# A hybrid decoder block on one core: MLP row tiles at another address, the start of the input norm in another order

## The chip, the cores and the metric

One Trainium2 chip, one NeuronCore of it. The metric is the device time of one execution in microseconds; of several runs the median is given. Five engines work side by side, each through its own list of instructions in order: TensorE (PE in the profile, PEld its weight loads), VectorE (DVE), ScalarE (ACT), GpSimd (POOL) and SyncE (SP, here only the queue that issues transfers). They wait for one another by semaphores.

## What is computed

One layer on a sequence of 512 rows of width 1024, float32 in and out:

```python
u = rmsnorm(h, norm_mix_pre_w)
proj = u @ w_in                       # q, k, v, z, xbc, dt_raw, gate_logits
att = dilated_window_attention(q, k, v) @ w_att_proj
ssm = mamba2_mixer(z, xbc, dt_raw, ...) @ w_ssm_proj    # a = -exp(a_log), dt from softplus(dt_raw + dt_bias)
g_att, g_ssm = split(sigmoid(gate_logits + b_gate))
h = h + rmsnorm((g_att * att + g_ssm * ssm) @ w_out, norm_mix_post_w)
f = rmsnorm(h, norm_ffn_pre_w)
f = square(relu(f @ w_up)) @ w_down   # 1024 -> 4096 -> 1024
h = h + rmsnorm(f, norm_ffn_post_w)
```

## The kernel before

**Products in three parts.** A float32 operand is split into a high part in a rounded format (names with h: `uh`, `wh_...`) and a remainder in the same format (names with l: `ul`, `wl_...`). ACT makes the high part by a copy, DVE (at places POOL) the remainder by a subtraction. A product is then three products of TensorE: high x high, high x remainder, remainder x high. One operand of each is loaded into the array and held (128 x 128), the other is streamed through (up to 512 columns).

**Weights.** They come in units of 1 MB into `ws` (two buffers) and are split into `wh` and `wl` (two buffers each). The order of the units is one list; a unit is loaded when the one two places ahead has been used.

**The start.** The 512 rows of x are four tiles of 128 rows, i = 0 to 3. For each, `square_u(i)` makes the mean square (ACT squares and sums; for tiles 0 and 1 ACT takes one half of the columns and DVE the other), and POOL raises it to the power -1/2. `norm_u(i)` multiplies on DVE, in two halves, for tiles 1 to 3 also by the norm's weight row (`row0`, which comes by transfer). `transpose_u` turns the eight 128 x 128 blocks on TensorE (`ut`), and `split_u0`/`split_u` cast them into `uh` and `ul`. Beside this run the first products, the attention values: `values(d, i)` multiplies tile i by the 256 columns of weight unit v1 (d = 1), then v0 (d = 0, with 32 columns more for dt), then v2, in eight steps k of three products each, into banks `psv`. The weights of v1 come in four quarters, and `split_v1(k)` splits the quarter for steps k and k + 1. The table `V_STEPS` says behind which step of which values the norm (n), the squares (s), the transposes (t) and others of later tiles are written. TensorE's list, and the instructions wrapped in `pin`, keep the order in which they are written; the rest is ordered by priority, the earlier written first.

Ahead of all this TensorE multiplies a tile of ones by itself `WARM` times into a bank `warm` that nobody reads. Each such product of 128 x 128 in full float32 is two pieces in the profile.

The small rows `dt_bias` and `a_log` come by transfer into `rows`; ACT takes the exponential of the second (L452). It isn't pinned.

**Middle.** Attention over 12 heads with the other input projections between (psq, psk, psga, psgs, psz), then the state-space mixer by eight groups (psx, psbc, pssp and small products), then the output projection (pso, psp).

**The MLP.** `fh` and `fl` hold the normed rows, transposed, for the up projection (psu, psuX and others). Its result stays in `hidden`, 32 tiles k of 128 features by 512 rows. For the down projection (psd) `hsplit(k)` splits one such tile into `hh` and `hl`; these rows are the operand held in the array, four slices of 128 rows each, and the weights `wh_dn` and `wl_dn` are streamed, 512 columns at a time, into eight banks (four row tiles by two halves). That makes 32 x 4 x 2 x 3 = 768 products. The last weight unit is split into tiles of its own, `wh_l` and `wl_l`. The tiles of k = 0 (`hs0`) lie in the pool `resid`, the others in the pools `hsplit` and `down`.

**Where the tiles lie.** Pools on one side are stacked: `resid` (residual rows, statistics, two or three scratch tiles), on it `fpool` (`fh`, `fl`), and once `fpool` is closed, in its place `down` (with `wh_l`, `wl_l`, `rowe`, the output tiles) and `hsplit`. `fpool` begins with an unused tile `fgap` of 104 floats, 416 bytes. With it `fh` and `fl` begin 480 bytes past a multiple of 512, as do `uh`, `ul`, the weight tiles `wh` and `wl`, and both operands of the output projection. `hh`, `hl`, `wh_l` and `wl_l` begin 64 bytes past one.

Of the kernel before, what the change touches and what calls it, by code (L numbers as in the profile page):

```python
# [11 lines left out]
F32 = mybir.dt.float32  # L12
F32R = mybir.dt.float32r
AF = mybir.ActivationFunctionType
# [4 lines left out]
P = 128  # L19
# [30 lines left out]
V_STEPS = {(1, 0, 2): (("s", 2),), (1, 0, 5): (("t", 1),), (1, 0, 6): (("n", 2),), (1, 1, 1): (("s", 3),),  # L50
           (1, 1, 3): (("t", 2),), (1, 1, 5): (("n", 3),), (1, 2, 3): (("t", 3), ("w", 0)), (1, 2, 7): (("p", 0),)}

WARM = 13
ATT_UNITS = ("q0", "k0", "ga0", "q1", "k1", "ga1", "q2", "k2", "ga2", "ga3", "gs0", "z0")


# [26 lines left out]
def hybrid_block(ctx: ExitStack, tc: tile.TileContext, a: dict):  # L83
    nc = tc.nc
    act, dve, pool, pe, sp = nc.scalar, nc.vector, nc.gpsimd, nc.tensor, nc.sync
# [75 lines left out]
    def v3(t, k):  # L161
        return t.rearrange("p (k n) -> p k n", k=k)
# [53 lines left out]
    ones = const.tile([P, P], F32, name="ones")  # L216
# [5 lines left out]
    def pin(ins):  # L222
        return tc.keep_in_program_order(ins)

    def mm(*args, **kw):
        tc.keep_in_program_order(pe.matmul(*args, **kw))  # L226
# [7 lines left out]
    def three(ps, wh, wl, uh, ul, start, stop, w_moving=False):  # L234
        if w_moving:
            mm(ps, uh, wh, start=start, stop=False)
            mm(ps, uh, wl, start=False, stop=False)
            mm(ps, ul, wh, start=False, stop=stop)
        else:
            mm(ps, wh, uh, start=start, stop=False)  # L240
            mm(ps, wh, ul, start=False, stop=False)
            mm(ps, wl, uh, start=False, stop=stop)
# [11 lines left out]
    def gbank(name):  # L254
        return psg.tile([P, T], F32, name=name, tag="g")
# [21 lines left out]
    with tc.tile_pool(name="start", bufs=1, reuse_waits="tile") as st:  # L277
# [8 lines left out]
        rows = st.tile([P, 2, SH], F32, name="rows")  # L286
# [28 lines left out]
        def square_u(i):  # L315
            un = uns[i] = st.tile([P, D], F32, name=f"un{i}", tag="un", bufs=2)
            if i < 2:
                pin(act.activation(un[:, :T], xt[:, i, :T], AF.Square, scale=RD, accum_out=sq0[:, i, 0:1]))
                pin(dve.tensor_scalar(sq0[:, i, 1:2], sq0[:, i, 0:1], EPS, None, ALU.add))
                pin(dve.tensor_tensor_reduce(un[:, T:], xt[:, i, T:], xt[:, i, T:], 1.0 / D, sq0[:, i, 1:2], ALU.mult,  # L320
                                             ALU.add, rs[:, i : i + 1]))
            else:
                pin(act.activation(un, xt[:, i, :], AF.Square, scale=RD, accum_out=ssq[:, i : i + 1]))
                pin(dve.tensor_scalar(rs[:, i : i + 1], ssq[:, i : i + 1], EPS, None, ALU.add))
            pin(pool.tensor_tensor(rs[:, i : i + 1], rs[:, i : i + 1], mhalf, op=ALU.pow))
# [10 lines left out]
        def transpose_u(i, b, banks=1):  # L336
            pt = [abank(f"ut{i}_{b}{n}") for n in range(banks)]
            for j in range(4):
                k = 4 * b + j
                tr(pt[j % banks][:, j * P : (j + 1) * P], uns[i][:, k * P : (k + 1) * P])  # L340
            pts[i, b] = pt[0]
            for j in range(4):
                pts[4 * b + j] = pt[j % banks][:, j * P : (j + 1) * P]

        def split_u0(k):
            hi = uh[:, k, 0:P]
            pin(act.activation(hi, pts[k], AF.Copy, scale=ncol[:, k : k + 1]))
            pin(dve.scalar_tensor_tensor(ul[:, k, 0:P], pts[k], ncol[:, k : k + 1], hi.bitcast(F32), op0=ALU.mult,
                                         op1=ALU.subtract))

        def split_u(i, b):
            p3 = pts.pop((i, b)).rearrange("p (k t) -> p k t", k=4)
            hi = uh[:, 4 * b : 4 * b + 4, i * P : (i + 1) * P]
            pin(act.activation(hi, p3, AF.Copy))
            pin(dve.tensor_tensor(ul[:, 4 * b : 4 * b + 4, i * P : (i + 1) * P], p3, hi.bitcast(F32), op=ALU.subtract))

        def split_v1(k, eng=dve):
            ks = slice(k * UC, (k + 2) * UC)
            pin(act.activation(wh1[:, ks], ws1[:, ks], AF.Copy))
            pin(eng.tensor_tensor(wl1[:, ks], ws1[:, ks], wh1[:, ks].bitcast(F32), op=ALU.subtract))  # L360

        def split_v0(k, eng=dve):
            ks = slice(k, k + 4)
            pin(act.activation(wh0[:, ks, :], ws0[:, ks, :], AF.Copy))
            pin(eng.tensor_tensor(wl0[:, ks, :], ws0[:, ks, :], wh0[:, ks, :].bitcast(F32), op=ALU.subtract))

        warm = gbank("warm")
        for _ in range(WARM):
            mm(warm[:, 0:P], ones, ones, start=True, stop=True)
        square_u(0)  # L370
        norm_u(0)
        transpose_u(0, 0, 2)
# [1 line left out]
        split_v1(0)  # L374
        split_u0(0)
        split_u0(1)
        square_u(1)
        split_v1(2)
        split_u0(2)
        split_u0(3)  # L380
        split_v1(4, pool)
        split_u0(4)
        split_u0(5)
        norm_u(1, (0,))
# [15 lines left out]
        def values(d, i):  # L400
            isl = slice(i * P, (i + 1) * P)
            n = VW if d == 0 else UC
            hi, lo = (wh0, wl0) if d == 0 else wv[d]
            ps = gbank(f"psv{d}_{i}")
            for k in range(KD):
                three(ps[:, :n], hi[:, k, :], lo[:, k, :], uh[:, k, isl], ul[:, k, isl],
                      k == 0, k == KD - 1, w_moving=True)
                yield
            act.activation(vtok[:, i, d * UC : (d + 1) * UC], ps[:, :UC], AF.Copy)
            if d == 0:  # L410
                dve.tensor_tensor(raw[:, i, :], ps[:, UC:VW], rows[:, 0, :], op=ALU.add)

        wv = {1: (v3(wh1, KD), v3(wl1, KD))}
        for d, i in V_ORDER:
            for k, _ in enumerate(values(d, i)):
                for step, n in V_STEPS.get((d, i, k), ()):
                    if step == "t":
                        transpose_u(n, 0)
                        transpose_u(n, 1)
                        split_u(n, 0)  # L420
                        split_u(n, 1)
                    elif step == "w":
                        split_v0(0)
                        split_v0(4, pool)
                    elif step == "p":
                        prep(0, 0)
                        wv[2] = [v3(t, KD) for t in take("v2")]
                    else:
                        (square_u if step == "s" else norm_u)(n)
# [19 lines left out]
        dve.tensor_scalar(t[0], t[0], 0.0, None, ALU.max)  # L449
        dve.scalar_tensor_tensor(dtp, t[3], 2.0, t[0], op0=ALU.mult, op1=ALU.add)  # L450

        act.activation(rows[:, 1, :], rows[:, 1, :], AF.Exp)  # L452
        for c in range(NT):
            dve.scalar_tensor_tensor(t[1][:, :, c, :], dtp[:, :, c, :], -1.0,
                                     rows[:, 1, :].rearrange("p (g h) -> p g h", g=GROUPS),
# [165 lines left out]
    for key in ATT_UNITS:  # L621
        n, j = key[:-1], int(key[-1])
# [303 lines left out]
    rp = ctx.enter_context(tc.tile_pool(name="resid", bufs=1, reuse_waits="tile"))  # L926
# [5 lines left out]
    rowf = ow.tile([P, D], F32, name="rowf", tag="rowf")  # L932
    sp.dma_start(rowf, a["norm_ffn_pre_w"].broadcast_to([P, D]))
    sm = rp.tile([P, 6, NT], F32, name="sm")

    fctx = ExitStack()
    fp = fctx.enter_context(tc.tile_pool(name="fpool", bufs=1, reuse_waits="tile"))
    fp.tile([P, 104], F32, name="fgap")
    fh = fp.tile([P, KD, T], F32R, name="fh")
    fl = fp.tile([P, KD, T], F32R, name="fl")  # L940

# [414 lines left out]
```

## Time and profile before

| | |
|---|---|
| median of 3 runs | 1108.18 us (1108.18 to 1108.34) |
| the profiled execution's own time | 1107.94 us |
| its span, first to last instruction | 1106.2 us |
| TensorE busy | 1092.2 us, 99% |
| VectorE, ScalarE, GpSimd busy | 726.7, 534.2, 63.8 us |
| mean granted TensorE clock | 0.998 |
| the down product's 768 products, first to last | 920 to 1099.5 us of the span |

A row of the chain of work reads: start, length, engine, tile, line, and how many instructions it holds; a row of groups: line, engine, operation, output<-inputs, shapes, count, then busy time and mean duration in ns, then the idle time of the engine ahead of them. The inputs' names stand in no particular order. A row of the timeline has start and length in us, and in brackets how long the engine was idle before it and what ended that. A row of windows has the stretch, its length, then for each engine (PE, PEld, DVE, ACT, POOL) its busy time and count, then the granted clock, the share of the transfer engines and GB/s. Products overlap, so the duration of one (near 390 ns) is longer than the step to the next (near 230 ns).

### The profile page before, as it was taken

The page shows a single profiled execution, that of the slowest core. Times are in us where ns is not written, and L with a number is a line of the kernel's source. Part 1 is how long each engine was busy: PE and PEld are TensorE (multiplying, and loading weights), DVE is VectorE, ACT ScalarE, POOL GpSimd, SP SyncE. Part 2 cuts the span into 40 slices and gives each one's busy share as a digit, 9 for nine tenths or more (in the row PEclk, how much of TensorE's full clock was granted, in tenths as well). Part 3 has the DMA queues.
Part 4 walks back from the last instruction along what each step waited for, and adds up shares of the span by engine and source line. Part 5 has one row for each costly group of instructions (what it writes and reads, how often), then busy time and mean ns, then how long its engine had stood idle before and what let it go on. Part 6 is the DMA issues. An engine that isn't in the chain of part 4 may idle for free.

```text
span 1106.2 us, 14632 instructions
## 1 busy us (share of the span) xinstructions
PE 1092.2 (99%) x5923; PEld 923.3 (83%) x5923; DVE 726.7 (66%) x1080; ACT 534.2 (48%) x943; POOL 63.8 (6%) x71
## 2 busy tenths in 40 slices
PE   8999999999999999999999999999999999999997
PEld 7988887778878888888888888889899998888886
DVE  5657666446776879696969695868577775332324
ACT  6356656445375654637373723454356764322211
POOL 2203222000000000000000000000000000000000
PEclk9999999999999999999999999999999999999999
DMA  8232222323323232332424223540323333232202
GB/s 276 80 103 81 58 66 67 105 68 104 115 77 115 77 114 77 115 99 93 136 80 127 77 79 112 192 150 2 114 85 107 116 115 133 77 136 93 87 29 76
DMA packets 86756, 110.92 MB, mean 100 GB/s; under 512 B 4240, under 2 KB 74384, under 8 KB 85664
## 3 DMA queue, kind: packets, MB, share of 16 engines
q1 hardware_dynamic: 85216, 101.01, 28.7%
q0 software_dynamic: 1328, 8.98, 2.1%
q8 instruction: 46, 0.75, 0.3%
q14 instruction: 22, 0.18, 0.1%
q10 hardware_dynamic: 144, 0.00, 0.0%
HBM read 107.82 MB, written 2.16 MB: 99 GB/s over the span
## 4 chain that ended last, share of the span: by engine, by line
PE 90%; DVE 4%; ACT 2%; DMA 2%; issue 1%; SPq 1%; POOL 0%; POOLq 0%; DVEq 0%; ACTq 0%
PE psd L226 16%; PE psz L226 8%; PE psx L226 8%; PE pssp L226 7%; PE psbc L226 6%; PE psuX L226 5%; PE psu L226 5%; PE psga L226 4%; PE psgs L226 4%; PE psk L226 3%; PE psq L226 3%; PE psap L226 3%; PE psv L226 3%; PE psuZ L226 3%; PE pq L226 1%; PE pyd L226 1%
## 5 line engine op out<-in xcount | busy, mean ns | idle before, releaser
L226 PE MATMUL psd<-wh_dn,hl 128*128 128x512 f32 x240 | 95.1, 396 | 0.0
L226 PE MATMUL psd<-wl_dn,hh 128*128 128x512 f32 x240 | 95.1, 396 | 0.0
L226 PE MATMUL psd<-wh_dn,hh 128*128 128x512 f32 x240 | 95.1, 396 | 0.0
L98 DVE TENSOR_TENSOR hl<-hidden,hh 128x512 fp32r<-128x512 f32 x32 | 21.9, 692 | 77.8 <-ACT hh L95 77.8
L95 ACT ACTIVATE hh<-hidden 128x512 fp32r<-128x512 f32 x32 | 19.8, 629 | 98.3 <-PE psd L226 98.2
L226 PEld LDWEIGHTS psd<-wh_dn,hl 128*128 128x128 f32 x240 | 45.2, 188 | 11.0
L226 PEld LDWEIGHTS psd<-wh_dn,hh 128*128 128x128 f32 x240 | 45.2, 188 | 10.9
L226 PEld LDWEIGHTS psd<-wl_dn,hh 128*128 128x128 f32 x240 | 45.2, 188 | 10.9
L226 PE MATMUL psbc<-uh,wh_bc 128*128 128x512 f32 x128 | 52.8, 413 | 0.0
L226 PE MATMUL pssp<-yth,wh_sp 128*128 128x512 f32 x128 | 51.4, 401 | 0.0
L226 PE MATMUL psz<-uh,wh_z 128*128 128x512 f32 x128 | 51.1, 399 | 0.0
L226 PE MATMUL psx<-uh,wl_x 128*128 128x512 f32 x128 | 49.9, 390 | 0.7 <-DVE wl_x L98 0.7
L226 PE MATMUL psx<-uh,wh_x 128*128 128x512 f32 x128 | 50.4, 394 | 0.0
L226 PE MATMUL psz<-uh,wl_z 128*128 128x512 f32 x128 | 50.2, 392 | 0.2 <-DVE wl_z L98 0.2
L686 DVE SCALAR_TENSOR_TENSOR ch<-psx,cw,ch 128x511 f32<-128x511 f32 (+2 forms) x48 | 35.9, 747 | 22.0 <-ACT ch L684 21.3
L226 PE MATMUL pssp<-yth,wl_sp 128*128 128x512 f32 x128 | 50.1, 392 | 0.0
L226 PE MATMUL pssp<-ytl,wh_sp 128*128 128x512 f32 x128 | 49.9, 390 | 0.0
L226 PE MATMUL psz<-ul,wh_z 128*128 128x512 f32 x128 | 49.9, 390 | 0.0
L226 PE MATMUL psbc<-uh,wl_bc 128*128 128x512 f32 x128 | 49.9, 390 | 0.0
L226 PE MATMUL psbc<-ul,wh_bc 128*128 128x512 f32 x128 | 49.8, 389 | 0.0
L226 PE MATMUL psx<-ul,wh_x 128*128 128x512 f32 x128 | 49.8, 389 | 0.0
L98 DVE TENSOR_TENSOR wl_dn<-ws_dn,wh_dn 128x2048 fp32r<-128x2048 f32 (+1 forms) x17 | 34.5, 2040 | 14.9 <-ACT wh_dn L95 14.9
(351 smaller groups left out, 3226.3 us busy)
## 6 DMA issues: line engine op xcount, KB each, us to landing
ws_up<-in_w_up_dram SPq DMA_DIRECT2D x16, 1024.0 KB, 5.6
ws_dn<-in_w_down_dram SPq DMA_DIRECT2D x15, 1024.0 KB, 5.0
ws_z<-in_w_in_dram SPq DMA_DIRECT2D x8, 1024.0 KB, 7.1
ws_x<-in_w_in_dram SPq DMA_DIRECT2D x8, 1024.0 KB, 5.3
w<-acs_d POOLq DMA_DIRECT2D x8, 1024.0 KB, 5.0
ws_bc<-in_w_in_dram SPq DMA_DIRECT2D x16, 512.0 KB, 4.8
ws_sp<-in_w_ssm_proj_dram SPq DMA_DIRECT2D x8, 1024.0 KB, 5.0
ws_ga<-in_w_in_dram SPq DMA_DIRECT2D x4, 1024.0 KB, 5.4
```

Of the source, the lines that this page charges most:

```text
L95: ins = act.activation(hi, src, AF.Copy)
L98: ins = (eng or dve).tensor_tensor(lo, src, hi.bitcast(F32), op=ALU.subtract)
L226: tc.keep_in_program_order(pe.matmul(*args, **kw))
L686: dve.scalar_tensor_tensor(h[:, d:], ps[:, : T - d], cw[:, ct, 3 - d : 4 - d], h[:, d:], op0=ALU.mult, op1=ALU.add)
```

## The change

It has four parts. The unused tile of 104 floats moves from `fpool` to `resid`, which lies under it: `fh` and `fl` stay at their addresses, while `hh`, `hl` (those of k = 0 too), `wh_l`, `wl_l`, the output tiles, `rowe` and the scratch tiles of `resid` move up by 416 bytes, from 64 to 480 past a multiple of 512. Constant products stand between the first value products: one more ahead of the start (`WARM`), and by `WARM_AT` 3, 2 and 2 behind steps 1, 3 and 5 of the first tile. In the input norm `square_u(1)` is written behind the casts of steps 2 and 3, and POOL makes the weight remainder of quarter 2 (steps 2, 3) where it made that of quarter 4. The exponential of `a_log` is pinned, which puts it where it is written.

```diff
--- before.py
+++ after.py
@@ -50,7 +50,8 @@
 V_STEPS = {(1, 0, 2): (("s", 2),), (1, 0, 5): (("t", 1),), (1, 0, 6): (("n", 2),), (1, 1, 1): (("s", 3),),
            (1, 1, 3): (("t", 2),), (1, 1, 5): (("n", 3),), (1, 2, 3): (("t", 3), ("w", 0)), (1, 2, 7): (("p", 0),)}
 
-WARM = 13
+WARM = 14
+WARM_AT = {1: 3, 3: 2, 5: 2}
 ATT_UNITS = ("q0", "k0", "ga0", "q1", "k1", "ga1", "q2", "k2", "ga2", "ga3", "gs0", "z0")
 
 
@@ -365,8 +366,12 @@
             pin(eng.tensor_tensor(wl0[:, ks, :], ws0[:, ks, :], wh0[:, ks, :].bitcast(F32), op=ALU.subtract))
 
         warm = gbank("warm")
-        for _ in range(WARM):
-            mm(warm[:, 0:P], ones, ones, start=True, stop=True)
+
+        def warm_up(n):
+            for _ in range(n):
+                mm(warm[:, 0:P], ones, ones, start=True, stop=True)
+
+        warm_up(WARM)
         square_u(0)
         norm_u(0)
         transpose_u(0, 0, 2)
@@ -374,11 +379,11 @@
         split_v1(0)
         split_u0(0)
         split_u0(1)
-        square_u(1)
-        split_v1(2)
+        split_v1(2, pool)
         split_u0(2)
         split_u0(3)
-        split_v1(4, pool)
+        square_u(1)
+        split_v1(4)
         split_u0(4)
         split_u0(5)
         norm_u(1, (0,))
@@ -413,6 +418,8 @@
         wv = {1: (v3(wh1, KD), v3(wl1, KD))}
         for d, i in V_ORDER:
             for k, _ in enumerate(values(d, i)):
+                if (d, i) == (1, 0):
+                    warm_up(WARM_AT.get(k, 0))
                 for step, n in V_STEPS.get((d, i, k), ()):
                     if step == "t":
                         transpose_u(n, 0)
@@ -449,7 +456,7 @@
         dve.tensor_scalar(t[0], t[0], 0.0, None, ALU.max)
         dve.scalar_tensor_tensor(dtp, t[3], 2.0, t[0], op0=ALU.mult, op1=ALU.add)
 
-        act.activation(rows[:, 1, :], rows[:, 1, :], AF.Exp)
+        pin(act.activation(rows[:, 1, :], rows[:, 1, :], AF.Exp))
         for c in range(NT):
             dve.scalar_tensor_tensor(t[1][:, :, c, :], dtp[:, :, c, :], -1.0,
                                      rows[:, 1, :].rearrange("p (g h) -> p g h", g=GROUPS),
@@ -932,10 +939,10 @@
     rowf = ow.tile([P, D], F32, name="rowf", tag="rowf")
     sp.dma_start(rowf, a["norm_ffn_pre_w"].broadcast_to([P, D]))
     sm = rp.tile([P, 6, NT], F32, name="sm")
+    rp.tile([P, 104], F32, name="gap")
 
     fctx = ExitStack()
     fp = fctx.enter_context(tc.tile_pool(name="fpool", bufs=1, reuse_waits="tile"))
-    fp.tile([P, 104], F32, name="fgap")
     fh = fp.tile([P, KD, T], F32R, name="fh")
     fl = fp.tile([P, KD, T], F32R, name="fl")
 
```

TensorE's list in the first values, from the last product of step 0 on; `psv1_0` is the bank of tile 0, `wh_v1`, `wl_v1` the weights, `uh`, `ul` the rows. Before:

```order
L226 MATMUL psv1_0_209<-wh_v1_109,ul_85 128x256 [waits DVE_49]
L226 MATMUL psv1_0_209<-wh_v1_109,uh_84 128x256 [waits Activation_49]
L226 MATMUL psv1_0_209<-wl_v1_110,uh_84 128x256
L226 MATMUL psv1_0_209<-wh_v1_109,ul_85 128x256 [waits DVE_49]
L226 MATMUL psv1_0_209<-wh_v1_109,uh_84 128x256 [waits Activation_49]
L226 MATMUL psv1_0_209<-wl_v1_110,uh_84 128x256 [waits DVE_49]
```

Now:

```order
L227 MATMUL psv1_0_210<-wh_v1_109,ul_85 128x256 [waits DVE_49]
L227 MATMUL psv1_0_210<-wh_v1_109,uh_84 128x256 [waits Activation_49]
L227 MATMUL psv1_0_210<-wl_v1_110,uh_84 128x256
L227 MATMUL psv1_0_210<-wh_v1_109,ul_85 128x256 [waits DVE_49]
L227 MATMUL warm_127<-ones_70 128x128 x3
L227 MATMUL psv1_0_210<-wh_v1_109,uh_84 128x256 [waits Activation_49]
L227 MATMUL psv1_0_210<-wl_v1_110,uh_84 128x256 [waits Pool_49]
```

Behind step 1 stand three constant products, and the product with the remainder of quarter 2 waits for POOL and not for DVE. (Behind steps 3 and 5 stand two each, and the remainder of quarter 4 now comes from DVE.)

ACT's list at the same place (`un1` is the scratch and later the normed tile 1, `sq0` its sum, `ut0_..` the transposed blocks of tile 0). Before:

```order
L347 ACTIVATE uh_84<-ut0_01_149,ncol_99 128x128 [waits PE_49]
L318 ACTIVATE un1_166,sq0_125<-xt_100 128x512 [waits DMAHW5_49]
L359 ACTIVATE wh_v1_109<-ws_v1_108 128x512 [waits DMAHW4_49]
L347 ACTIVATE uh_84<-ut0_00_148,ncol_99 128x128 [waits DVE_49]
L347 ACTIVATE uh_84<-ut0_01_149,ncol_99 128x128 [waits DVE_49]
L359 ACTIVATE wh_v1_109<-ws_v1_108 128x512 [waits DMAHW7_49]
```

Now:

```order
L348 ACTIVATE uh_84<-ut0_01_150,ncol_99 128x128 [waits PE_49]
L360 ACTIVATE wh_v1_109<-ws_v1_108 128x512 [waits DMAHW4_49]
L348 ACTIVATE uh_84<-ut0_00_149,ncol_99 128x128 [waits DVE_49]
L348 ACTIVATE uh_84<-ut0_01_150,ncol_99 128x128 [waits DVE_49]
L319 ACTIVATE un1_173,sq0_125<-xt_100 128x512 [waits DMAHW5_49]
L360 ACTIVATE wh_v1_109<-ws_v1_108 128x512 [waits DMAHW7_49]
```

The square of tile 1 stands behind a weight cast and two row casts. On DVE its sum, the other half's squares and the remainder of a weight quarter likewise follow two row remainders that stood behind them.

POOL's list (`rs` is raised to the power -1/2; `cw`, `cb` are constants of the convolution). Before:

```order
L325 TENSOR_TENSOR rs_126<-rs_126,mhalf_68 128x1 [waits DVE_49,Pool_49]
L325 TENSOR_TENSOR rs_126<-rs_126,mhalf_68 128x1 [waits DVE_49]
L360 TENSOR_TENSOR wl_v1_110<-ws_v1_108,wh_v1_109 128x512 [waits DMAHW7_49,Activation_49]
L325 TENSOR_TENSOR rs_126<-rs_126,mhalf_68 128x1 [waits DVE_49] x2
L431 TENSOR_SCALAR cw_199<-cw_199 128x128 [waits DMAHW4_49]
L431 TENSOR_SCALAR cb_201<-cb_201 128x32 [waits DMAHW5_49]
```

Now:

```order
L326 TENSOR_TENSOR rs_126<-rs_126,mhalf_68 128x1 [waits DVE_49,Pool_49]
L361 TENSOR_TENSOR wl_v1_110<-ws_v1_108,wh_v1_109 128x512 [waits DMAHW4_49,Activation_49]
L326 TENSOR_TENSOR rs_126<-rs_126,mhalf_68 128x1 [waits DVE_49] x3
L438 TENSOR_SCALAR cw_200<-cw_200 128x128 [waits DMAHW4_49]
L438 TENSOR_SCALAR cb_202<-cb_202 128x32 [waits DMAHW5_49]
```

The weight remainder stands ahead of tile 1's power.

ACT's list where the exponential stood (`ut2_..` and `ut3_..` are the transposed tiles 2 and 3, `vtok` the values evacuated from their banks). Before:

```order
L323 ACTIVATE un3_262,ssq_124<-xt_100 128x1024 [waits DMAHW4_49,DVE_49]
L452 ACTIVATE rows_105<-rows_105 128x32 [waits DMAHW0_49]
L354 ACTIVATE uh_84<-ut2_00_272 128x4x128 [waits PE_49]
L354 ACTIVATE uh_84<-ut2_10_277 128x4x128 [waits PE_49]
L409 ACTIVATE vtok_89<-psv1_1_255 128x256 [waits PE_49]
L354 ACTIVATE uh_84<-ut3_00_314 128x4x128 [waits PE_49]
```

Now, there:

```order
L414 ACTIVATE vtok_89<-psv1_0_210 128x256 [waits PE_49]
L324 ACTIVATE un3_270,ssq_124<-xt_100 128x1024 [waits DMAHW4_49,DVE_49]
L355 ACTIVATE uh_84<-ut2_00_280 128x4x128 [waits PE_49]
L355 ACTIVATE uh_84<-ut2_10_285 128x4x128 [waits PE_49]
L414 ACTIVATE vtok_89<-psv1_1_263 128x256 [waits PE_49]
L355 ACTIVATE uh_84<-ut3_00_322 128x4x128 [waits PE_49]
```

and where it now stands, behind the exponential of dt and between evacuations of values:

```order
L414 ACTIVATE vtok_89<-psv0_2_441 128x256 [waits PE_49]
L414 ACTIVATE vtok_89<-psv0_3_468 128x256 [waits PE_49]
L447 ACTIVATE dt1_619<-dt1_619 128x128 [waits DVE_49]
L459 ACTIVATE rows_105<-rows_105 128x32 [waits DMAHW0_49]
L414 ACTIVATE vtok_89<-psv2_0_495 128x256 [waits PE_49]
L414 ACTIVATE vtok_89<-psv2_1_521 128x256 [waits PE_49]
```

Tile 2's casts follow the square of tile 3 directly; the exponential comes seven evacuations later.

## The prediction

> **What bounds the kernel now.** I read the page's share of busy time first, then the chain that ended last, then the groups of matrix products by shape, and last the first 30 us as a timeline, because the change touches only the start and the addresses of the last stage.
>
> ```profile
> span 1106.2 us, 14632 instructions
> PE 1092.2 (99%) x5923; PEld 923.3 (83%) x5923; DVE 726.7 (66%) x1080; ACT 534.2 (48%) x943; POOL 63.8 (6%) x71
> PE 90%; DVE 4%; ACT 2%; DMA 2%; issue 1%; SPq 1%; POOL 0%; POOLq 0%; DVEq 0%; ACTq 0%
> ```
>
> The kernel is a string of products on TensorE; other engines carry a tenth of the chain. So two things can move the time: the step from one product to the next where TensorE is never kept waiting, and the few waits at the start. The chain gives that step directly, since a piece of it is a stretch of products without a gap (start, length, count):
>
> ```profile
> 244.37 10.88 PE psx L226 x48
> 676.60 16.36 PE psgs L226 x72
> 740.37 5.49 PE psp L226 x24
> 920.17 174.16 PE psd L226 x744
> ```
>
> All four are 512 columns wide in the same number type. One step is 226.7 ns in psx, 227.2 in psgs, 228.8 in psp, but 174.16 / 744 = 234.1 ns in psd, the down product of the MLP. The groups by shape (busy, mean ns of one) say the same in another way:
>
> ```profile
> L226 PE MATMUL psd<-wl_dn,hh 128*128 128x512 f32 x240 | 95.1, 396 | 0.0
> L226 PE MATMUL psd<-wh_l,hh 128*128 128x512 f32 x16 | 6.2, 390 | 0.0
> L226 PE MATMUL psd<-wl_l,hh 128*128 128x512 f32 x16 | 6.3, 394 | 0.0
> L226 PE MATMUL pso<-wh_o,mh 128*128 128x512 f32 x32 | 12.4, 389 | 0.0
> L226 PE MATMUL psbc<-uh,wh_bc 128*128 128x512 f32 x128 | 52.8, 413 | 0.0
> ```
>
> The pso products have the psd's form (weights streamed, rows held) and take 389 ns against 396. What differs is the layout: in pso, psx, psgs and psp both operands begin 480 bytes past a multiple of 512. In psd the streamed wh_dn and wl_dn do so too, but the held hh and hl begin at 64. In the last weight pair both wh_l and hh begin at 64, and those rows, in the same stage, lie between (390 and 394). So the trace shows the dear step with unequal residues, cheaper ones with equal residues.
>
> **The layout's price.** The change puts hh, hl, wh_l and wl_l at 480 like the rest; fh and fl stay where they were. No instruction is added. All 768 products of the stage lie on the chain, with no idle time ahead of them (0.0), so what a step saves the end saves. 744 x (234.1 - 227.0) = 5.3 us; the other 24, part of them the cheaper last pair, give some 0.1. Together 5.4 us. I take 227.0, between psx and psgs, since these are stretches without a break. The ends: psp, with transposes just ahead of it, gives 744 x 5.3 = 3.9 us; psx gives 5.6; if equal residues only bring what the wh_l and wl_l rows show (393 on average, 3 under 396), 768 x 3 ns = 2.3 us. A faster stage needs a new pair of weight tiles every 10.9 us (48 products) and not every 11.2; the psd piece runs 174 us with no other engine in it, so loads and casts have room for these 3%.
>
> The Trainium skill (TensorE: Matmul & The Clock Gate, "Step-by-step: what each phase is for") says the opposite of a layout effect: two independent read ports, one for the streamed operand and one for weights, so "Loading the next tile's weights doesn't steal SBUF read bandwidth from the running matmul." By that rule this part brings 0 and the sum keeps only the start, 1106.7; the rows 396 and 389 for one form disagree with it, or at least show something it leaves out.
>
> **The start: clock and norm of tile 1.** Four windows (length, busy time and count by engine, granted clock):
>
> ```profile
> 8.80:12.21 3.41, 1.97 (x12) 1.48 (x12) 3.11 (x9) 2.86 (x9) 2.19 (x2) 1.00 0.98 332
> 12.21:15.63 3.42, 3.00 (x15) 2.60 (x14) 2.61 (x7) 2.03 (x4) 0.55 (x1) 0.50 1.06 379
> 15.63:19.04 3.41, 3.41 (x30) 3.28 (x30) 2.13 (x5) 1.62 (x4) 0.56 (x1) 1.00 0.63 179
> 916.75:920.16 3.41, 2.53 (x21) 2.33 (x20) 3.41 (x7) 1.45 (x3) 0.00 (x0) 1.00 0.20 41
> ```
>
> TensorE was busy 1.97 of 3.41 us, and in the next window its clock is 0.50; after 3.00 it is 1.00 again. A window with 2.53 later in the kernel is followed by no drop. So somewhere between 1.97 and 2.53 busy lies the point at which the clock falls. The rows of that time:
>
> ```profile
> 1.16 5.17 PE L226 MATMUL warm<-ones 128*128 128x128 f32 x26 [1.16 <-POOL ones L217]
> 6.37 1.09 PE L229 MATMUL ut<-ident,un 128*128 128x128 f32 x8
> 7.72 0.63 ACT L318 ACTIVATE un<-xt 128x512 f32<-128x512 f32 x1
> 8.35 0.62 ACT L359 ACTIVATE wh_v<-ws_v 128x512 fp32r<-128x512 f32 x1
> 8.48 0.15 DVE L319 TENSOR_SCALAR sq<-sq 128x1 f32<-128x1 f32 x1 [0.21 <-ACT un L318]
> 9.51 0.94 POOL L325 TENSOR_TENSOR rs<-rs,mhalf 128x1 f32<-128x1 f32 x1 [3.71 <-DVE rs L320]
> 10.41 1.28 POOL L360 TENSOR_TENSOR wl_v<-ws_v,wh_v 128x512 fp32r<-128x512 f32 x1
> 11.37 0.88 DVE L333 SCALAR_TENSOR_TENSOR un<-xt,rs,row 128x512 f32<-128x512 f32 x1 [0.30 <-issue]
> 13.29 0.74 DVE L333 SCALAR_TENSOR_TENSOR un<-xt,rs,row 128x512 f32<-128x512 f32 x1
> 14.08 1.12 PE L229 MATMUL ut<-ident,un 128*128 128x128 f32 x4 [0.42 <-DVE un L333]
> 14.99 0.69 DVE L355 TENSOR_TENSOR ul<-ut,uh 128x512 fp32r<-128x512 f32 x1 [0.33 <-ACT uh L354]
> 15.87 0.69 DVE L355 TENSOR_TENSOR ul<-ut,uh 128x512 fp32r<-128x512 f32 x1 [0.19 <-ACT uh L354]
> 16.47 1.40 DVE L333 SCALAR_TENSOR_TENSOR un<-xt,rs,row 128x512 f32<-128x512 f32 x2
> ```
>
> Step by step. One more constant product ahead: two more pieces, at 5.17 / 26 = 0.2 us each at most; they end about where the transposes start (6.37), so 0 to 0.1. ACT squares tile 1 behind a weight cast and two row casts, about 0.9 later (8.6 for 7.72), so DVE's row of 8.48 comes at 9.34. DVE works from 8.48 to 11.07 on what precedes the first half of tile 1's norm (11.37, after 0.30 idle); two row remainders of 0.26 each now go ahead of it. 9.34 + 2.59 - 0.52 = 11.41, against 11.37: nothing lost, because the 0.30 of idle covers it; were that cover absent, 0.3 would be. POOL makes the weight remainder (1.28) ahead of its power (0.94): it can begin at 8.2, once ACT has cast them, and end at 9.5, before the power's input comes at 10.3 (9.34 + 0.15 + the 0.75 or so of the other half's squares). TensorE gets its third and fifth weight remainders some 0.6 and 0.8 us earlier.
>
> The seven constant products (14 pieces, some 0.11 us each at full clock, 1.6 in all) stand where TensorE waits anyway: 3 while the third weights are made, 2 and 2 before tile 1's norm. They end before the first half arrives at 12.3, cost nothing on the path, and lift 1.97 above 3. So 12.21 to 15.63 runs at full clock. That is worth little: DVE ends tile 1's norm at 14.07 for 14.03, the four transposes then take 0.55 (half of the 1.09 for eight) for 1.12, and the second DVE remainder can start no sooner than 0.60 behind 14.99: 15.59 for 15.87. Norm of tile 2 and what follows come 0.28 earlier.
>
> **The exponential.**
>
> ```profile
> 18.35 0.36 PE L226 MATMUL psv<-wh_v,uh 128*128 128x256 f32 x1
> 19.49 0.23 ACT L452 ACTIVATE rows<-rows 128x32 f32<-128x32 f32 x1 [1.88 <-DMA rows<-in_a_log_dram]
> 19.63 1.07 ACT L354 ACTIVATE uh<-ut 128x512 fp32r<-128x512 f32 x2
> 20.24 1.29 DVE L355 TENSOR_TENSOR ul<-ut,uh 128x512 fp32r<-128x512 f32 x2 [2.30 <-ACT uh L354]
> 20.26 0.39 PE L226 MATMUL psv<-wh_v,uh 128*128 128x256 f32 x1 [0.24 <-ACT uh L354]
> 20.99 0.39 PE L226 MATMUL psv<-wh_v,ul 128*128 128x256 f32 x1 [0.22 <-DVE ul L355]
> 21.45 1.41 DVE L333 SCALAR_TENSOR_TENSOR un<-xt,rs,row 128x512 f32<-128x512 f32 x2
> 22.28 1.35 PE L229 MATMUL ut<-ident,un 128*128 128x128 f32 x8
> 23.38 0.37 PE L226 MATMUL psv<-wh_v,uh 128*128 128x256 f32 x1
> 26.45 2.80 POOL L365 TENSOR_TENSOR wl_v<-ws_v,wh_v 128x1152 fp32r<-128x1152 f32 x1 [3.49 <-ACT wh_v L364]
> 29.52 0.29 PE L226 MATMUL psv<-wl_v,uh 128*128 128x288 f32 x1
> ```
>
> ACT stands 1.88 us for a small transfer, with tile 2's casts queued behind it; DVE waits 2.30 for them, then TensorE for both. Without the exponential there, ACT casts tile 2 from about 18.3. TensorE would be at the next tile at 18.35 + 12 x 0.12 = 19.8 (the window at 15.63 holds 30 products and transposes in 3.41, 0.11 to 0.12 each), not 20.26 (0.4); its product with the remainder follows 0.24 behind and not at 20.99 (0.5); the transposes of tile 3 no longer wait for DVE's norm (22.28 to 23.38 is 1.1, eight take 0.9: 0.2), and 0.1 of uneven steps goes. With the 0.25 from the clock TensorE reaches the product of 23.38 at 21.9: 1.45 us. What is late next: POOL's weight remainder ends at 29.25 and TensorE uses it at 29.52. It moves along, for it hangs on ACT behind tile 3's transposes; if it did not, 1.2 of the 1.45 would be lost there. In its new place the exponential (0.23) stands on ACT ahead of the evacuations of the last four value tiles. With three banks TensorE needs an evacuated bank only two tiles later, some 5 us; that is its cover, and without it the cost would be 0.23. No DMA is moved, and nothing on SP's queue. Ends for the whole start: 0.3 and 1.7.
>
> **Sum.** Profiled execution 1107.94 (1.74 around its span): 1107.94 - 5.4 - 1.45 = 1101.1. The median of the runs, 1108.18, is 0.24 above that execution, so 1101.3.
>
> **The rivals.** *The clock falls one window later.* From 12.21 to 15.63 TensorE would wait from about 12.9 to 14.1 for the norm: 2.2 busy, between 1.97 and 2.53, the gap in which the drop sits. Then 15.63 to 19.04 is at half clock; working the same rows at twice the step, TensorE is about 0.9 late at 18.35, the exponential's gain absorbs most, and 0.3 stays: 1102.5. For it: those 2.2 are nearer to 1.97. Against: 8 transposes and 8 products run in it at full clock, where the earlier window had 12 products. The Trainium skill (the same page, "Part 4: PE-mode transpose") says that transposes do not count as busy in the same way, which would favour this rival; no row here separates them. That page's table for the clock ("What's actually happening") lets the clock drop only after an idle window; by it neither window would have dropped, and the trace's 1.97 busy followed by 0.50 disagrees.
>
> *Equal residues bring only the last pair's rows.* 2.3 instead of 5.4: 1104.4. For it: that pair is the only one in this stage with equal residues. Against: it is mixed with unequal ones.
>
> *The layout does nothing*, and 234.1 has another cause, such as the stage's transfers and casts: only the start remains, 1106.7. Against it: the wh_l rows at 390 in the same stage.
>
> *Equal residues at 480 are themselves dear* (ends slower). The first product of each triple at 480 takes 413 in psbc. If the down stage took that for a third of its products, 256 x 17 ns = 4.4 us more, less 1.45: 1111.1. It decides from 410 ns on. Against it: pso at 389.
>
> **How the numbers follow.** The forecast 0.50, clock one window later 0.25, last pair's rows 0.10, layout nothing 0.12, 480 dear 0.03. A measurement of this kernel tells about 0.2% (2.2 us) from no change: the first three are faster, 0.85; layout nothing is the same, 0.12; slower 0.03. The range goes from 1100.5 (5.6 and 1.7, without the 0.24) to the last pair's 1104.4, which leaves 0.15 out.
>
> **What would show it.** A psd piece of the chain at 227 ns a step and groups at 389 to 390; no half clock in 12.21 to 15.63, nor after; no wait of ACT on the a_log transfer; the first 288-column product at 26.3 for 27.8. A psd step still at 234, or a half clock at 15.63, makes me wrong.

## The result, and the profile after

| | before | after |
|---|---|---|
| median of 6 runs | 1108.09 us (1107.58 to 1108.34) | 1101.12 us (1100.69 to 1101.41, and one run of 1545.77) |
| the profiled execution's own time | 1107.94 us | 1101.41 us |
| its span | 1106.2 us | 1099.6 us |
| TensorE busy | 1092.2 us | 1086.6 us |

After to before is 0.9937, with a 95% interval of 0.9924 to 0.9951: 7 us less. The run of 1545.77 us had a mean clock of 0.654 over its whole length and stands outside that ratio; the median without it is 1100.99.

The head of the page of after:

```profile
span 1099.6 us, 14665 instructions
PE 1086.6 (99%) x5939; PEld 923.9 (84%) x5939; DVE 725.3 (66%) x1080; ACT 534.5 (49%) x943; POOL 63.9 (6%) x71
```

The same four stretches of the chain as in the prediction (start, length, count), now of after:

```profile
243.21 10.88 PE psx L227 x48
675.52 16.36 PE psgs L227 x72
739.44 5.49 PE psp L227 x24
919.22 168.68 PE psd L227 x744
```

Two differences to read. The psd piece takes 168.68 us for 174.16: one step is 168.68 / 744 = 226.7 ns, the step of psx, so the dear step is gone. And psd starts at 919.22 for 920.17: 0.95 came from the start in this execution. 5.48 + 0.95 is nearly all of the span's 6.6; what stands behind the piece, its last 24 products among it, gives most of the rest. psx, psgs and psp keep their lengths to the last digit.

The groups by shape of after (busy, mean ns of one):

```profile
L227 PE MATMUL psd<-wl_dn,hh 128*128 128x512 f32 x240 | 93.4, 389 | 0.0
L227 PE MATMUL psd<-wh_dn,hl 128*128 128x512 f32 x240 | 93.4, 389 | 0.0
L227 PE MATMUL psbc<-uh,wh_bc 128*128 128x512 f32 x128 | 52.9, 413 | 0.0
```

396 became 389, while psbc's 413, which a rival took for the price of the place 480, stands as it stood.

The start. Rows of after's timeline:

```profile
6.80 1.04 PE L230 MATMUL ut<-ident,un 128*128 128x128 f32 x8
8.55 1.28 POOL L361 TENSOR_TENSOR wl_v<-ws_v,wh_v 128x512 fp32r<-128x512 f32 x1 [2.86 <-ACT wh_v L360]
9.63 0.15 DVE L320 TENSOR_SCALAR sq<-sq 128x1 f32<-128x1 f32 x1 [0.26 <-ACT un L319]
11.63 0.75 DVE L334 SCALAR_TENSOR_TENSOR un<-xt,rs,row 128x512 f32<-128x512 f32 x1
13.42 0.74 DVE L334 SCALAR_TENSOR_TENSOR un<-xt,rs,row 128x512 f32<-128x512 f32 x1
17.71 1.26 ACT L355 ACTIVATE uh<-ut 128x512 fp32r<-128x512 f32 x2 [0.67 <-PE ut L230]
21.83 0.36 PE L227 MATMUL psv<-wh_v,uh 128*128 128x256 f32 x1
26.23 0.30 PE L227 MATMUL psv<-wh_v,uh 128*128 128x288 f32 x1
28.27 0.40 PE L227 MATMUL psv<-wl_v,uh 128*128 128x288 f32 x1
```

ACT casts tile 2 at 17.71, released by the transposes and no longer by the a_log transfer (19.63 before). The product of 23.38 stands at 21.83, the first of 288 columns at 26.23 for 27.78: 1.55 earlier. But the first product that needs POOL's remainder of v0, the fifth with a weight remainder, begins at 28.27, 1.25 earlier than the 29.52 of before; it stands 0.43 us behind the product before it, where the step is 0.13, so 0.3 us are lost there. POOL's rows say why:

```profile
23.65 0.54 POOL L438 TENSOR_SCALAR cw<-cw 128x128 f32<-128x128 f32 x1 [5.33 <-DMA cw<-in_conv_w_dram]
24.16 1.20 POOL L438 TENSOR_SCALAR cb<-cb 128x32 f32<-128x32 f32 x1
25.32 0.25 POOL L438 TENSOR_SCALAR bg<-bg 128x16 f32<-128x16 f32 x1
25.54 2.68 POOL L366 TENSOR_TENSOR wl_v<-ws_v,wh_v 128x1152 fp32r<-128x1152 f32 x1
```

ACT had made the input of L366 by 24.87 (2.22 us from 22.65), but POOL's list has three small products on constants ahead of it, and the transfer of cw came at 23.65; before it came at 21.18.

The granted clock, window by window (length, busy time and count of PE, PEld, DVE, ACT, POOL, clock):

```profile
9.66:13.07 3.41, 3.18 (x23) 2.79 (x23) 3.37 (x10) 2.12 (x6) 1.11 (x2) 1.00 1.02 372
13.07:16.48 3.41, 2.32 (x19) 2.12 (x19) 2.71 (x6) 3.02 (x6) 0.55 (x1) 1.00 1.04 333
16.48:19.90 3.42, 3.42 (x30) 3.18 (x29) 2.77 (x6) 1.86 (x5) 0.55 (x1) 1.00 0.61 195
```

No half clock behind the window of 3.18, and none behind the one of 2.32. The windows are not where they were: in before the clock rose first at 5.39 us of the span, here at 6.24.

### The profile page after: what moved, and what is told of

Read it like the earlier page. It is cut to its first block, busy times and chain, and to the rows that moved or that the text cites. A ratio compares the mean times of both kernels' runs of the same rounds, so it can differ in the third digit from the quotient of the medians.

```text
span 1099.6 us, 14665 instructions
## 1 busy us (share of the span) xinstructions
PE 1086.6 (99%) x5939; PEld 923.9 (84%) x5939; DVE 725.3 (66%) x1080; ACT 534.5 (49%) x943; POOL 63.9 (6%) x71
## 4 chain that ended last, share of the span: by engine, by line
PE 89%; DVE 4%; ACT 2%; DMA 1%; issue 1%; POOL 1%; POOLq 0%; DVEq 0%; ACTq 0%
PE psd L227 15%; PE psz L227 8%; PE psx L227 8%; PE pssp L227 8%; PE psbc L227 6%; PE psuX L227 5%; PE psu L227 5%; PE psga L227 4%; PE psgs L227 4%; PE psk L227 3%; PE psq L227 3%; PE psap L227 3%; PE psuZ L227 3%; PE psv L227 2%; PE pq L227 1%; PE pyd L227 1%
```

## The experiments

Two theories were to be told apart first: that the address of the MLP's rows is the cause of the dear step, and that the start had somehow changed the stage; then which part of the start pays, and what about the address counts.

### Each half by itself

**The layout alone**, on the kernel before:

```diff
     sm = rp.tile([P, 6, NT], F32, name="sm")
+    rp.tile([P, 104], F32, name="gap")
...
-    fp.tile([P, 104], F32, name="fgap")
```

> Only the unused tile of 104 floats moves; the start is that of before. If the address is the cause of the dear step: psd piece of the chain 168 to 169 us (226.7 ns a step), psd start unchanged at 920.2, time 1108.1 - 5.5 = 1102.6. If the layout does nothing and the start changed the stage (for instance by the clock's phase): 174 us in the psd piece, 1108.1. If only like residues of the last pair count: 1105.8.

**The start alone**: the changed kernel with these two lines put back.

> All changes at the start, the layout as before. If the two parts are independent: the psd piece stays at 174.2 us (234.1 ns a step), psd starts at 919.0 to 919.3 where it started at 920.17, time 1108.1 - 1.1 = 1107.0. If the start also acts on the stage: psd piece under 173. The wait for the late remainder at 28 us is expected again if it hangs on the instruction order (first wl_v product with 288 columns at 28.3), and gone (27.9) if it came from one late transfer of that execution.

**The exponential alone**, on the kernel before:

```diff
-        act.activation(rows[:, 1, :], rows[:, 1, :], AF.Exp)
+        pin(act.activation(rows[:, 1, :], rows[:, 1, :], AF.Exp))
```

> Before, with the exponential pinned and nothing else. If the exponential carries the start's gain: no wait of ACT on a_log, the first 288-column product at 26.6 for 27.78 and psd start at 919.2 to 919.5, time 1107.2. If most of the gain came from the clock window (half clock from 12.2 to 15.6 before): psd start 920.0, time 1107.9.

The last piece of the chain (start, length, count), with the layout alone:

```profile
920.70 168.68 PE psd L226 x744
```

With the start alone:

```profile
918.79 174.16 PE psd L227 x744
```

And with the exponential alone:

```profile
918.94 174.16 PE psd L226 x744
```

| | median, us | to before (1107.95, 21 runs) | ratio, 95% |
|---|---|---|---|
| layout alone | 1102.54 (5 runs) | -5.41 | 0.9951 [0.9939, 0.9964] |
| start alone | 1106.59 (11 runs) | -1.36 | 0.9987 [0.9978, 0.9996] |
| exponential alone | 1106.70 (11 runs) | -1.25 | 0.9989 [0.998, 0.9998] |

The halves add up, within the noise: 5.41 + 1.36 = 6.77, of the 6.97 measured together. The psd piece is 168.68 with the layout and 174.16 without it, whatever the start. The exponential alone brings 1.25 of the 1.36, and the intervals can't tell these two apart. Both kernels started psd earlier than expected (918.79 for 919.0 to 919.3, 918.94 for 919.2 to 919.5) and ended 0.4 to 0.5 us sooner than expected. The wait of TensorE at 28 us, seen in the changed kernel, is in neither profile. Two more lines, of the timelines, show how the exponential acts. ACT's exponential in the kernel with the layout alone:

```profile
20.02 0.23 ACT L452 ACTIVATE rows<-rows 128x32 f32<-128x32 f32 x1 [2.82 <-DMA rows<-in_a_log_dram]
```

ACT's casts of tile 2 in the kernel with the exponential alone:

```profile
18.11 1.26 ACT L354 ACTIVATE uh<-ut 128x512 fp32r<-128x512 f32 x2 [0.54 <-PE ut L229]
```

The first of these two kernels has the start of before, and ran this time without a half clock in the start. ACT was free earlier, at 17.2 instead of 17.6, and waited 2.82 us instead of 1.88, since the transfer set the time. psd then started even later than in before, 920.70 for 920.17. So full clock ahead of that wait bought nothing in this execution. The runs of before fit it: of the 21, the four with a mean clock of 1.000 took 1107.56 to 1108.48 us, the six with 0.996 or 0.997 took 1107.62 to 1108.76.

### The a_log transfer early

The kernel before, with the transfer on another queue and the exponential pinned at its old place:

```diff
         act.dma_start(ncol, a["norm_mix_pre_c"])
+        act.dma_start(rows[:, 1, :], a["a_log"].broadcast_to([P, SH]))
...
                         (square_u if step == "s" else norm_u)(n)
+                        if (step, n) == ("s", 3):
+                            pin(act.activation(rows[:, 1, :], rows[:, 1, :], AF.Exp))
```

> Before, with a_log loaded at the start on ACT's own queue, behind ncol, and the exponential pinned where it stood, between the square of tile 3 and the casts of tile 2. Nothing else changes. If ACT's wait for that small transfer is the price: exponential at 17.6 without a wait, psd start at 919.1 to 919.4, time as with the pinned exponential plus up to 0.2, 1106.7 to 1107.0. If its place between the casts is the price: 1108.

Measured: 1107.46 us (11 runs), ratio 0.9996 [0.9987, 1.0005]. Three rows of it, the first transposes, the exponential and the casts of tile 2:

```profile
7.91 1.09 PE L229 MATMUL ut<-ident,un 128*128 128x128 f32 x8 [2.15 <-DVE un L332]
18.10 0.22 ACT L431 ACTIVATE rows<-rows 128x32 f32<-128x32 f32 x1
18.79 1.26 ACT L355 ACTIVATE uh<-ut 128x512 fp32r<-128x512 f32 x2 [0.47 <-PE ut L229]
```

The wait is gone, and so is most of the gain: the first transposes stand at 7.91 and not at 6.37, because DVE's norm of tile 0 came later. From there to the start of psd (919.69) it is 911.8 us, against 913.8 before and 912.5 with the exponential pinned alone. Behind the exponential ACT still waited 0.47 us for the transposes, so its place ahead of these casts delayed nothing. By this one trace the wait was the price and the place was not; the time alone doesn't show it, since its interval includes no change, and both numbers expected for the first case, 919.1 to 919.4 and 1106.7 to 1107.0, were missed. The late start came from the input: DVE's squares of tile 0 began at 5.87 us, after 1.50 us of waiting for the transfer of x, where they began at 4.22 to 4.92 in the other thirteen profiles. That the added early transfer held it up fits, and no run here isolates it.

### The constant products alone

The changed kernel with `WARM = 13` and `WARM_AT = {}`, and beside it the changed kernel once more.

> After without the constant products (one fewer ahead, none between the first values); order, exponential and layout stay. If they are worth what the prediction gave them (the clock, 0.25): 1101.4, and a window with under 2 us of TensorE work near 9 to 12 us followed by one at half clock in most executions. If they cost as much as they bring: 1101.1 or a little less. If the clock matters more than thought: over 1102.

> The changed kernel once more, for a second execution on the same chip as the others. Time 1101.1; psd piece 168.7 us. If the wait at 28.27 for POOL's late remainder hangs on when the cw transfer lands, the first execution's 0.44 us gap need not come again, and psd then starts at 918.7 to 918.9; if it belongs to the order, it comes again.

Measured on the same chip: 1101.02 us without the constant products (five runs: 1100.79, 1100.95, 1101.02, 1102.05, 1102.42), 1101.10 with them (1100.52 to 1101.37). The medians are equal. The mean granted clock goes with the time here: the three short runs had 0.998 or 0.999, the two long ones 0.995. The drop that was expected in most executions is not in the profiled one, a short run: its windows of 2.92, 2.44 and 2.21 us of TensorE work from 5.87 us on are all at full clock. With the constant products no run of the changed kernel was under 0.998 but that of 1545.77, nor any of the start alone. With the exponential alone, which has no constant products either, six of eleven were at 0.996 or 0.997, and among them were the three longest, 1107.18 to 1107.70; its mean is 1106.81 against 1106.54 for the whole start, which has the other order too. So these products are worth nothing in the middle run; the means differ by 0.3 and 0.5 us, and the two long runs are 1.0 to 1.4 above the median. That such runs are those with half clock in the start is argued and not shown: none of the long runs without constant products has a profile, and the mean clock also counts the kernel's end, where TensorE is idle (0.998 in the second profile of the changed kernel, with half clock in its last microseconds and none in the start).

The second profiled execution of the changed kernel started psd at 918.49, not 919.22. POOL there got cw at 22.69, its remainder waited for ACT, and the wait at 28 us was absent:

```profile
25.12 2.80 POOL L366 TENSOR_TENSOR wl_v<-ws_v,wh_v 128x1152 fp32r<-128x1152 f32 x1 [1.43 <-ACT wh_v L365]
```

In all nine profiles with this order and these lists POOL got cw between 21.24 and 23.65 us, and only in the first, with 23.65, did its remainder wait for that. So the wait belongs to that execution and not to the order.

### POOL's three small products behind the remainder

```diff
         for t in (cw, cb_, bg):
-            pool.tensor_scalar(t, t, 0.5, None, ALU.mult)
+            pin(pool.tensor_scalar(t, t, 0.5, None, ALU.mult))
```

> After, with POOL's three small products of cw, cb and bg pinned, which puts them behind the weight remainder of v0 on POOL. If POOL's late start (25.54, behind a late cw transfer) is why TensorE waited at 28.27: POOL begins the remainder at 24.9, ends at 27.6, the first wl_v product with 288 columns starts at 27.97, and the time is 0.3 below after, 1100.8. If something else is late there, the product stays at 28.27 and the time at 1101.1.

Measured: 1100.99 us (5 runs), ratio 0.9937 [0.9923, 0.995]. POOL began the remainder as soon as its input was there, with nothing ahead of it:

```profile
25.29 2.81 POOL L366 TENSOR_TENSOR wl_v<-ws_v,wh_v 128x1152 fp32r<-128x1152 f32 x1 [6.64 <-ACT wh_v L365]
28.18 1.39 POOL L438 TENSOR_SCALAR cw<-cw 128x128 f32<-128x128 f32 x1
```

No wait of TensorE is left there; the tiles came a little later in this execution (the first 288-column product at 26.57 for 26.23), so the product that uses the remainder stood at 28.31 and the expected 27.97 was not met. It takes a chance away rather than time: 0.1 us in the medians, which can't be told from none.

### Which distance between the two operands counts

Three kernels share the 416 bytes of the gap differently between the two pools, so that `fh` and `fl` stay and of the products' operands only `hh`, `hl`, `wh_l`, `wl_l` move:

```diff
-    rp.tile([P, 104], F32, name="gap")
+    rp.tile([P, 40], F32, name="gap")
...
+    fp.tile([P, 64], F32, name="fgap")
     fh = fp.tile([P, KD, T], F32R, name="fh")
```

(and 72 with 32, 96 with 8).

> After, with 40 floats of the gap in resid and 64 in fpool: hh, hl, wh_l, wl_l at 224 past a multiple of 512, the other weights at 480, distance 256 bytes. If places must be equal modulo 512: psd step 234 ns, piece 174.2 us, time 1106.6. If modulo 256 or less is enough: 226.7 ns, 168.7 us, 1101.1.

> After, with 72 floats of the gap in resid and 32 in fpool: hh, hl, wh_l, wl_l at 352 past a multiple of 512, the other weights at 480, distance 128 bytes. If places must be equal modulo 256 or 512: psd step 234 ns, piece 174.2 us, 1106.6. If modulo 128 or less is enough: 226.7 ns, 168.7 us, 1101.1.

> After, with 96 floats of the gap in resid and 8 in fpool: hh, hl, wh_l, wl_l at 448 past a multiple of 512, the other weights at 480, distance 32 bytes. If places must be equal modulo 64 or more: psd step 234 ns, piece 174.2 us, 1106.6. If the cost grows with the distance (before: 96 bytes, 7.4 ns a step): 229 ns, 170.6 us, 1103.

The psd piece of the chain with 40 floats (held rows at 224):

```profile
918.02 168.68 PE psd L227 x744
```

With 72 floats (at 352):

```profile
918.84 172.81 PE psd L227 x744
```

With 96 floats (at 448):

```profile
918.42 173.53 PE psd L227 x744
```

| held rows at, modulo 512 | distance to the streamed weights' 480 | step, ns | time, one run |
|---|---|---|---|
| 480 (after) | 0 | 226.7 | 1101.1 (median) |
| 224 | 256 | 226.7 | 1100.19 |
| 352 | 128 | 232.3 | 1105.23 |
| 448 | 32 | 233.2 | 1105.56 |
| 64 (before) | 96 | 234.1 | 1108.1 (median) |

A distance of 256 bytes is as good as none. 128, 96 and 32 are dear, with little between them; it is neither a matter of 128-byte places nor one that grows with the distance. The three single runs were taken on another chip, where before took 1107.30 us, so the steps are to be compared and not the times with the two medians.

### The other weights moved

The last two moves show whether the rule belongs to psd or to all products. First all tiles of one side of the memory by 96 bytes:

```diff
+    const.tile([P, 24], F32, name="pad")
     acs_d = dram.tile([P, P], F32, name="acs_d")
```

> After, with an unused tile of 24 floats at the end of the constants' pool, which moves all tiles of that side by 96 bytes: weight tiles, fh, fl, hh, hl, wh_l, wl_l from 480 to 64 past a multiple of 512. The products of psd and of all psu groups then have both operands at 64 (2028 products); those of psq, psk, psga, psgs, psz, psap, psx, pssp (1968 of 512 columns) and psbc (384) have the held or the streamed weights at 64 and the other operand, uh, ul or att, still at 480. If equal places within 512 bytes are what counts: psd piece stays at 168.7 us, psx piece of 48 goes from 10.88 to 11.24, psgs piece of 72 from 16.36 to 16.86, time 1101.1 + 1968 x 7.4 ns = 1115.7, with psbc 1118.5. If only the address 480 is good: psd piece 174.2 too, and psu as well, 1130 to 1133. If only where hh and hl lie counts (64 bad for them alone): psd 174.2 and psx unchanged, 1106.6.

The chain of it, as above:

```profile
246.31 11.24 PE psx L227 x48
686.85 16.86 PE psgs L227 x72
714.95 22.41 PE pso L227 x96
751.87 5.48 PE psp L227 x24
931.65 168.68 PE psd L227 x744
```

One run gave 1113.81 us (before on the same chip: 1107.30). psd, with both operands now at 64, stays at 168.68: the place 480 itself is nothing special. psx and psgs, whose lengths were the same in all other kernels here, grow by exactly what was expected, 234.2 ns a step. psp, with both at 480, doesn't move. The expectation leaves out pso, whose streamed weights moved while its held rows did not: it has psd's form, and its 96 products take 22.41 us, 233.4 ns a step, where they took 21.76, 226.7 ns, in the kernel with 40 floats. The whole grew by 12.4 us up to the start of psd and not by 14.6 to 17.4: some of these groups took more than 226.7 ns already (in after psz's three groups have 399, 392 and 390 ns, and here 405, 397 and 395), so it seems that the expectation counted 7.4 ns for products that had only 5 or 6 to lose.

Then `fh` and `fl` alone, streamed in the up products, from 480 to 64, by an unused tile of 24 floats ahead of them:

> After, with an unused tile of 24 floats at the start of fpool: fh and fl, streamed in the up products, at 64 past a multiple of 512 and the held weights at 480; psd keeps 480 and 480. Of the 1260 products, some 144 are 512 columns wide, the rest 256. If the cost belongs to wide products alone: 144 x 7.4 ns = 1.1 us, steps of the 256-column products still 120 ns, psd start at 920.3, time 1102.2. If narrow products pay in proportion: steps of 124 ns, 1116 x 3.7 ns = 4.1 us more, 1106.3.

Groups of it by shape, and last one of after:

```profile
L227 PE MATMUL psu<-fh,wh_up 128*128 128x512 f32 x48 | 19.2, 399 | 0.0
L227 PE MATMUL psu<-fl,wh_up 128*128 128x512 f32 x48 | 18.8, 392 | 0.0
L227 PE MATMUL psu<-fl,wh_up 128*128 128x256 f32 x64 | 18.0, 282 | 0.0
L227 PE MATMUL psuX<-fl,wh_winb 128*128 128x256 f32 x88 | 24.9, 283 | 0.0
L227 PE MATMUL psu<-fh,wh_up 128*128 128x512 f32 x48 | 18.7, 389 | 0.0
```

In after all three groups of 512 columns have 389, and the narrow ones 283 to 285. The wide products pay, the narrow ones don't. The stretch from the start of psp to that of psd is 180.74 us, against 179.78 in after: 0.96, near the 1.1 expected for 144 products, so nothing is left for the 1116 narrow ones. The run gave 1101.42 and not 1102.2: it came to psp 0.9 earlier than that profile of after.

## Why the prediction was right, point by point

1. *The layout's price*, 5.4: measured 5.41 by the layout alone, 5.48 in the trace for the 744 products of the piece, and some 0.15 behind it, near the 0.1 taken for the other 24. Choosing an unbroken stretch (psx, psgs) for the step, and not psp, was the right choice; the step came out at psx's 226.7, below the 227.0 taken.
2. *The reason given for it*, equal residues modulo 512, was right in kind and too narrow by one step: equal modulo 256 is enough. The outcome that was weighed against it, 1106.7, is contradicted by 174.16 against 168.68 us with nothing but addresses changed. It was drawn from the two independent read ports of the Trainium skill (TensorE: Matmul & The Clock Gate, "Step-by-step: what each phase is for"), by which loading weights takes no read bandwidth from a running product; no run here shows what the two operands share.
3. *The start*, 1.45: 1.36 by the start alone (1.42 between the layout alone, 1102.54, and the whole change, 1101.12). The share of the exponential held: 1.25 by itself for 1.2. How that 1.2 splits into its parts (0.4, 0.5, 0.2, 0.1) no run separates. The 0.25 from clock and norm, read as an earlier second remainder in one execution's windows, came in the first profile of after (tile 2's norm at 16.22 for 16.47) but not in the medians: 0.1 is left for them there, which can't be told from none. That the sum still came out within 0.2 us is in part luck.
4. *Norm of tile 1 nothing lost*: DVE ended it at 14.16 for 14.03. The head of after was 0.4 later (first transposes at 6.80, since the clock rose later and the constant products ran longer, to 6.96), and the order gave it back. The price of one more constant product, 0 to 0.1, was therefore too low for this execution. Where the clock rises earlier it is nothing (in the start alone, with the rise at 5.22 us, the transposes waited for DVE's norm), but 28 pieces at half clock can end behind the norm of tile 0.
5. *POOL's remainder "moves along"*, because it hangs on ACT: this held in eight of the nine profiles with this order, and the condition for it was left out, that the constants' transfers land in time. In the first profile of after they hadn't, and 0.3 of the 1.55 was lost there. The sentence that no DMA is moved didn't rule this out: the transfer of cw was issued at 16.57 us as before (16.56), and POOL got it at 23.65 for 21.18. Over the executions the landing varies, 21.24 to 23.65 in those nine and 20.22 to 21.91 in four with the old order.
6. *The range.* Its lower bound follows from 1107.94 - 5.6 - 1.7, which is 1100.6 and not 1100.5; the measured time lies above both.
7. *The rivals.* The clock one window later did not come in the profiled executions with the constant products; the window that the prediction put at 2.2 held 2.04 to 2.53. The last pair's rows alone (1104.4), no effect of the layout (1106.7) and 480 itself dear (1111.1) are excluded by the layout alone (1102.54); that the place 480 is neither good nor bad by itself is shown by the kernel with both operands of psd at 64.

## What to carry to other kernels

Where products of 512 columns follow one another without a gap, compare the step (length of the piece over its count) between stages of one form: 226.7 and 234.1 ns looked alike among 390-ns durations, and 3% of a stage of 174 us was to be had by moving a tile, here with the streamed and the held rows a multiple of 256 bytes apart. A small transfer that an engine waits for in mid-list can cost all that is queued behind it, and hide what is gained ahead of it. Here moving its user behind the urgent work brought 1.25 us, while sending the transfer earlier brought nothing that could be measured. What a half clock costs has to be read from the spread of runs, not from one profile.

## What the runs showed of the hardware

**Addresses of the two operands.** With 512 columns an unbroken step is 226.7 ns where the streamed and the held rows begin a multiple of 256 bytes apart (0 or 256), and 232 to 234 ns at distances of 32, 96 and 128. With 256 columns no difference shows at the one place tried, 64 against 480 (281 to 285 ns a product either way). Each distance other than 0 and 96 rests on one run. Why is open: no run here looks inside.

**Where the clock drops.** Two of the fourteen profiles have a half clock in the start, before and the exponential alone, each behind a window with little work. The windows of the kernel with the exponential alone, the one ahead of the drop and the drop itself:

```profile
8.52:11.93 3.41, 1.77 (x10) 1.28 (x10) 2.73 (x9) 3.06 (x9) 2.19 (x2) 1.00 0.91 312
11.93:15.35 3.42, 2.96 (x14) 2.56 (x14) 2.59 (x7) 1.63 (x3) 0.44 (x1) 0.50 1.05 393
```

The least work between values and norm that was followed by full clock, in the kernel with POOL's products moved, and the window behind it:

```profile
11.23:14.65 3.42, 2.04 (x15) 1.62 (x15) 2.68 (x6) 2.05 (x5) 0.04 (x1) 1.00 1.03 401
14.65:18.06 3.41, 3.31 (x27) 2.86 (x25) 2.83 (x6) 2.58 (x8) 0.55 (x1) 1.00 0.79 223
```

In the start 1.77 and 1.97 were followed by a drop, 2.04, 2.20 and 2.32 not, which would put the point near 0.6 of a window (2.0 of 3.41 us). Busy time alone doesn't decide it, though. In the kernel with the early a_log transfer the first window behind the rise held 1.55, as this row says, and no drop came.

```profile
4.21:7.62 3.41, 1.55 (x14) 1.36 (x13) 1.16 (x4) 0.55 (x1) 0.55 (x1) 1.00 0.79 257
```

Nor does it at the end of the kernel. The last window with products held 1.66 us in after (1091.67 to 1095.08) and 1.57 in the kernel with 72 floats, and the next was at full clock; behind 1.44 in the kernel without constant products it was at half. What else counts is open.

The Trainium skill (TensorE: Matmul & The Clock Gate, "What's actually happening") lets the clock fall after an idle window. Behind the empty window of after, from 1095.08 to 1098.50 us, it did fall; the windows with 1.77 and 1.97 busy, behind which it fell too, were not idle. The same section says that the windows run freely, without regard to the kernel; the first rise, at 4.2 to 6.8 us of the span in these profiles, agrees, and it fits that one kernel has executions with and without the drop.
